# Two small experts of a mixture of experts computed in 21 short steps among the large ones, in place of four long blocks

## The chip, the cores and the metric

The kernel runs on one core of a Trainium2 chip. The metric is device microseconds (us) from the first to the last instruction of one execution, with what lies around it; several executions are timed and the median counts. The engines of the core work side by side, each through its own list of instructions in order: PE (matrix multiply; PEld is its weight load), DVE (elementwise), ACT (activations and copies), POOL, and SP, which here only issues the weight transfers (DMA).

## The reference

Two layers of a diffusion transformer on 256 latent and 256 context tokens, D_MODEL 1024. Only the end of the second layer is touched: the mixture of eight experts, of which each token takes two.

```python
def moe_swiglu(h, router, w_gate, w_up, w_down):
    ...
    top_val, top_idx = lax.top_k(logits, TOP_K)          # 2 of 8
    top_w = jax.nn.softmax(top_val, axis=-1)
    ...
    for e in range(N_EXPERTS):
        he = jax.nn.silu(t @ w_gate[e]) * (t @ w_up[e])   # 1024 -> 3584
        out = out + gates[:, e:e + 1] * (he @ w_down[e])  # 3584 -> 1024
```

All weights are float32; the eight experts' gate, up and down matrices are 352 MB, each read once.

## The kernel before

The mixture fills the second half of the span. The router sorts experts 2 to 7 by how many tokens chose them. The first six in processing order are **large**: up to 128 token rows each, computed with split weights. `eload` (L157 to L164) brings a **unit** of weights, 128 x 2048 float32 or 1 MB, into one of eight ring buffers (`w` four times, `x1w` and `zw` twice each) by a DMA on SP's queue. `wsplit` (L166) makes of each half of the unit a high part `wh` (ACT, L196) and a low part `wl` (DVE, L197); there are four buffers of each, two units' worth, so ACT and DVE can be two units ahead of PE. `mm3` (L185) then runs three matmuls: high by `wh` (L186), low by `wh` (L187), high by `wl` (L188).

The hidden width of 3584 is cut into four **pieces**: three of 1024 and one of 512 (`piece`). `up_big` does for a piece eight units of gate and up (four in the short one) into banks `mgu`: gate first, then up. `hidden` forms silu(gate) on ACT (L1810) and the product with up on DVE (L1811), tile `hd`. `turn` transposes `hd` on PE (`mht`, L1857) and splits it into `mdH` and `mdL`. `down_big` runs the down projection of the piece before (`yb`), four units. So the loop runs: gate and up of piece i, down of piece i-1, transposes of piece i. When a large expert is done, `finish` and `scatter` (`sct`) add its rows to `acc`; for every second expert `gather` (`xg`) collects the next two experts' rows.

The last two experts, the **pair**, have few tokens: 64 rows each. They share a 128-row tile: expert i's matmuls use half of PE's columns (`r = slice(64 * i, 64 * i + 64)`), unsplit, straight from the ring buffers. `up_pair` (`pgu`, L1844), `turn` with `pair` set (`mht`, tile `hTP`) and `down_pair` (`py`, L1887, sums in `yP` by L1893 and L1895) do a piece of both experts in one block of 24 units (16 of gate and up, 8 of down; half of that in the last piece). The four blocks stand in the list of tasks at fixed places:

```python
tasks = [(s, c) for s in range(PAIR) for c in range(NP)]
for c, i in zip(range(NP), (2, 8, 14, 20)):
    tasks.insert(i, (PAIR, c))
```

The code's order is not quite the engines' order: a scheduler in the framework, which estimates times when the kernel is built, lists every engine's instructions, and on the chip each engine follows its list. PSUM has four banks for gate and up (tag `gu`).

Of the kernel before, what the change touches and what calls it, by code (L numbers as in the profile page):

```python
# [17 lines left out]
P = 128  # L18
# [10 lines left out]
def build(tc, A, out, stages=("s0", "mix0", "ffn0", "mix1", "moe"), dbg=None):  # L29
# [1243 lines left out]
            T.matmul(b[:, 0:NE], ones, sel[:, t, :], start=(t == 0), stop=(t == 1))  # L1273
        V.tensor_copy(R_["cnt"], b[:, 0:NE])

    def route_order(tp, m2):


        n = NE - 2
        cnt, posm, gate = R_["cnt"], R_["posm"], R_["gate"]  # L1280
        sh = [P, n, n]

        def scr(nm):
            return m2.tile([P, n, n], F32, name="or" + nm, tag="or" + nm, bufs=1)
        a, q = scr("H"), scr("L")
        co = cnt[:, 2:].unsqueeze(1).to_broadcast(sh)
        ce = cnt[:, 2:].unsqueeze(2).to_broadcast(sh)
        V.tensor_tensor(q, co, ce, op=OP.is_equal)
        V.tensor_tensor(a, co, ce, op=OP.is_gt)
        V.tensor_tensor(q, q, R_["tie"][:, 2:, 2:], op=OP.mult)  # L1290
        V.tensor_tensor(a, a, q, op=OP.add)
        rank = tp.tile([P, n], F32, name="orank")
        V.tensor_reduce(rank, a, axis=AX.X, op=OP.add)

        one = tp.tile([P, n, n], F32, name="oone")
        V.scalar_tensor_tensor(one, rank.unsqueeze(1).to_broadcast(sh), 1.0,
                               iota[:, 0:n].unsqueeze(2).to_broadcast(sh), OP.add, OP.is_equal)

        def by_place(dst, src):
            q = scr("L")  # L1300
            V.tensor_tensor(q, one, src.unsqueeze(1).to_broadcast(sh), op=OP.mult)
            V.tensor_reduce(dst, q, axis=AX.X, op=OP.add)
        R_["posS"] = tp.tile([P, 2, n], F32, name="posS")
        R_["gateS"] = tp.tile([P, 2, n], F32, name="gateS")
        num = tp.tile([P, n], F32, name="onum")
        numi = tp.tile([P, n], I32, name="onumi")
        by_place(num, iota[:, 1:1 + n])
        V.tensor_copy(numi, num)
        for t in range(2):
            by_place(R_["posS"][:, t, :], posm[:, t, 2:])  # L1310
            by_place(R_["gateS"][:, t, :], gate[:, t, 2:])
        cap = R_["cap"] = tp.tile([P, NE], F32, name="ocap")
        G.memset(cap[:, 0:2], float(P))
        V.tensor_scalar(cap[:, 2:], rank, float(n - 2) - 0.5, -64.0, OP.is_gt, OP.mult)
        V.tensor_scalar(cap[:, 2:], cap[:, 2:], float(P), None, OP.add)
        return [nc.values_load(numi[0:1, i:i + 1], engines=[mybir.EngineType.SP], min_val=0, max_val=NE - 1)
                for i in range(n)]
# [391 lines left out]
    if "moe" in stages:  # L1709
# [27 lines left out]
        if True:  # L1737
# [64 lines left out]

                return c * 1024, min(1024, FFE - c * 1024)

            def hidden(bs):

                hds_ = []
                for g, u in zip(*bs):
                    hd = hd_tile()
                    S.activation(hd, g, AF.Silu)  # L1810
                    V.tensor_tensor(hd, u, hd, op=OP.mult)  # L1811
                    hds_.append(hd)
                return hds_

            def up_big(s, c, xH, xL, so):
                o, w = piece(c)
                nh, nk = w // 512, 2048 // w
                bs = []
                for i, W in enumerate((Wg, Wu)):
                    bb = [bank("mgu", "gu", 4) for _ in range(nh)]  # L1820
                    for u in range(KD // nk):
                        get = first.pop((s, c, i, u), None) or wsplit(eload(W, num[s], nk * u, o, w))
                        for h in range(nh):
                            for kk in range(nk):
                                k = nk * u + kk
                                mm3(bb[h], xH[:, k, so:so + P], xL[:, k, so:so + P],
                                    *get(kk * w + h * 512, 512), k == 0, k == KD - 1)
                    bs.append(bb)
                return hidden(bs)

            def up_pair(c, xP):
                o, w = piece(c)
                nh, nk = w // 512, 2048 // w
                bs = []
                for W in (Wg, Wu):
                    bb = [bank("pgu", "gu", 4) for _ in range(nh)]
                    for u in range(KD // nk):
                        ws = [eload(W, num[PAIR + i], nk * u, o, w) for i in range(2)]
                        for kk in range(nk):
                            k = nk * u + kk  # L1840
                            for h in range(nh):
                                for i in range(2):
                                    r = slice(64 * i, 64 * i + 64)
                                    T.matmul(bb[h][r], xP[:, k, r], ws[i][:, kk * w + h * 512:kk * w + h * 512 + 512],  # L1844
                                             start=(k == 0), stop=(k == KD - 1))
                    bs.append(bb)
                return hidden(bs)

            def turn(hds_, pair):

                n = 512 * len(hds_)
                dH = m2.tile([P, 1024], F32 if pair else F32R, tag="mdH", name="hTP" if pair else "mdH", bufs=1)
                dL = None if pair else m2.tile([P, 1024], F32R, tag="mdL", name="mdL", bufs=1)
                for j, hd in enumerate(hds_):
                    b = bank("mht", "mt", 1)
                    for f in range(4):
                        T.transpose(b[:, f * P:(f + 1) * P], hd[:, f * P:(f + 1) * P], ident)  # L1857
                    cs = slice(j * 512, (j + 1) * 512)
                    if pair:
                        S.activation(dH[:, cs], b, AF.Copy)  # L1860
                    else:
                        split_to(dH[:, cs], dL[:, cs], b)
                return dH, dL

            def down_big(s, c, dH, dL, yb):
                o, w = piece(c)
                for u in range(w // 256):
# [4 lines left out]
                    for f2, h in order:  # L1872
# [1 line left out]
                        fs = slice(f * P, (f + 1) * P)  # L1874
                        mm3(yb[h], dH[:, fs], dL[:, fs], *get(f2 * 1024 + h * 512, 512),
                            c == 0 and f == 0, c == NP - 1 and f == w // P - 1)

            def down_pair(c, hT, yP):
                o, w = piece(c)
                bb = [bank("py", "gu", 4) for _ in range(2)]  # L1880
                for u in range(w // 256):
                    ws = [eload(Wd, num[PAIR + i], o // P + 2 * u, 0, 1024) for i in range(2)]
                    for f2 in range(2):
                        f = 2 * u + f2
                        for h in range(2):
                            for i in range(2):
                                T.matmul(bb[h][64 * i:64 * i + 64], hT[:, f * P + 64 * i:f * P + 64 * i + 64],  # L1887
                                         ws[i][:, f2 * 1024 + h * 512:f2 * 1024 + (h + 1) * 512],
                                         start=(f == 0), stop=(f == w // P - 1))
                for h in range(2):  # L1890
                    cs = slice(h * 512, (h + 1) * 512)
                    if c:
                        V.tensor_tensor(yP[:, cs], bb[h], yP[:, cs], op=OP.add)  # L1893
                    else:
                        S.activation(yP[:, cs], bb[h], AF.Copy)  # L1895

            def scatter(acc, s, yH, yL):
                for t in range(2):
# [25 lines left out]
            xs_, SelT, ybs = {}, {}, {}  # L1924
            xs_[0] = gather(0)
            dump("lg", R_["lg"])
            tasks = [(s, c) for s in range(PAIR) for c in range(NP)]
            for c, i in zip(range(NP), (2, 8, 14, 20)):
                tasks.insert(i, (PAIR, c))
            tasks.append(None)  # L1930
            pend, done, yP = None, [], None
            for i, task in enumerate(tasks):
                hd_ = None
                if task is not None:
                    s, c = task
                    if s == PAIR:
                        hd_ = up_pair(c, xP)
                    else:
                        if c == 0:
                            ybs[s] = [bank("yb", "yb") for _ in range(2)]  # L1940
                        hd_ = up_big(s, c, *xs_[s // 2], (s % 2) * P)
                for d in done:
                    scatter(acc, *d)
                done = []
                if pend is not None:
                    (s1, c1), d1 = pend
                    if s1 == PAIR:
                        if c1 == 0:
                            yP = m2.tile([P, D], F32, name="yP", bufs=1)
                        down_pair(c1, d1[0], yP)  # L1950
                        if c1 == NP - 1:
                            done.append(finish(PAIR, yP))
                    else:
                        down_big(s1, c1, *d1, ybs[s1])
                        if c1 == NP - 1:
                            done.append(finish(s1, ybs.pop(s1)))
                pend = (task, turn(hd_, s == PAIR)) if task is not None else None
                if i == 0:
                    route_gates(mp, m2)
                    dump("gate", gate)  # L1960
                    num += route_order(mp, m2)
                    xP, gp = gather_pair()
                if i == 1:
                    acc = mp.tile([P, 2, D], F32, tag="acc", name="acc")
                    G.memset(acc, 0.0)
# [123 lines left out]
```

## Time and profile before

| what | us |
|---|---|
| median of three runs | 2022.61 (2021.28 to 2024.07) |
| the profiled execution | 2018.54 |
| its span, first to last instruction | 2016.8 |
| of which mixture of experts, first `mgu` to last `yb` | about 1047 to 1999 |
| PE busy over the span | 1860.4 |

Busy PE time is to be read with care: a matmul's row lasts longer than the distance to the next one, since they overlap. Work is therefore priced below by the distance between starts.

### The profile page before, as it was taken

What the parts mean: (1) busy time and instruction counts of PE and PEld (TensorE: products, weight loads), DVE (VectorE), ACT (ScalarE), POOL (GpSimd) and SP (SyncE); (2) the same over time, 40 slices, a digit from 0 to 9 for tenths busy, and PEclk for the clock granted to TensorE, in tenths of its full rate; (3) what the DMA queues carried; (4) which work ended last, traced back from release to release, by engine and by line L of the source; (5) the groups of instructions that cost most, each with busy time, mean ns of one, the idle gap of its engine ahead of it and who ended that gap; (6) DMA issues with size and microseconds to landing.
All of it is one profiled execution on the core that took longest, in us unless ns stands there. A gap on an engine that the chain in (4) does not pass through costs nothing. (4 is left out here: it accounts for less than half of the span.)

```text
span 2016.8 us, 25616 instructions
## 1 busy us (share of the span) xinstructions
PE 1860.4 (92%) x9278; PEld 1369.1 (68%) x9278; DVE 1394.2 (69%) x2054; ACT 1037.2 (51%) x1492; POOL 160.2 (8%) x144
## 2 busy tenths in 40 slices
PE   5999999989999999865879999999999999999996
PEld 2667667867777787655658467846785687567775
DVE  6575775688875476486778358935883588578886
ACT  3522355543333365325466347724772477457765
POOL 1000310001111001055220000000000000000000
PEclk9999999989999999887979999999999999999998
DMA  9474314436666656637557999899999999999992
GB/s 350 162 261 149 134 42 176 160 112 212 219 209 201 221 188 245 233 121 272 211 223 261 368 409 397 332 356 410 405 368 378 413 384 360 340 385 352 355 336 109
DMA packets 196970, 545.55 MB, mean 271 GB/s; under 512 B 32620, under 2 KB 62421, under 8 KB 189285
## 3 DMA queue, kind: packets, MB, share of 16 engines
q1 hardware_dynamic: 165884, 514.73, 68.2%
q10 hardware_dynamic: 29400, 23.50, 4.0%
q0 software_dynamic: 1552, 5.62, 1.0%
q8 instruction: 75, 1.23, 0.2%
q14 instruction: 59, 0.48, 0.1%
HBM read 517.85 MB, written 25.89 MB: 270 GB/s over the span
## 5 line engine op out<-in xcount | busy, mean ns | idle before, releaser
L197 DVE TENSOR_TENSOR wl<-w,wh 128x1024 fp32r<-128x1024 f32 x380 | 449.7, 1224 | 101.7 <-ACT wh L196 98.9
L196 ACT ACTIVATE wh<-w 128x1024 fp32r<-128x1024 f32 x390 | 395.4, 1055 | 190.8 <-PE dn L187 49.0
L186 PE MATMUL mgu<-wh,xgH 128*128 128x512 f32 x448 | 178.4, 399 | 0.0
L187 PE MATMUL mgu<-wh,xgL 128*128 128x512 f32 x448 | 176.8, 396 | 0.0
L188 PE MATMUL mgu<-wl,xgH 128*128 128x512 f32 x448 | 168.4, 399 | 0.9 <-DVE wl L197 0.7
L196 ACT ACTIVATE wh<-zw 128x1024 fp32r<-128x1024 f32 x122 | 124.3, 1057 | 53.5 <-DMA zw<-in_od_moe_w_down_dram 29.3
L197 DVE TENSOR_TENSOR wl<-x1w,wh 128x1024 fp32r<-128x1024 f32 x122 | 142.9, 1218 | 11.4 <-ACT wh L196 11.0
L186 PE MATMUL gu<-hH,wh 128*128 128x512 f32 (+1 forms) x384 | 146.9, 383 | 2.2 <-ACT hH L196 2.2
L197 DVE TENSOR_TENSOR wl<-zw,wh 128x1024 fp32r<-128x1024 f32 x122 | 142.4, 1218 | 7.9 <-ACT wh L196 7.6
L188 PE MATMUL gu<-hL,wh 128*128 128x512 f32 (+1 forms) x384 | 145.2, 379 | 0.0
L187 PE MATMUL gu<-hH,wl 128*128 128x512 f32 (+1 forms) x384 | 144.3, 376 | 0.0
L196 ACT ACTIVATE wh<-x1w 128x1024 fp32r<-128x1024 f32 x124 | 126.0, 1056 | 19.6 <-PE yb L187 6.9
L186 PE MATMUL yb<-wh,mdH 128*128 128x512 f32 x336 | 133.5, 398 | 0.7 <-ACT mdH L196 0.7
L187 PE MATMUL yb<-wh,mdL 128*128 128x512 f32 x336 | 132.4, 394 | 0.0
L188 PE MATMUL yb<-wl,mdH 128*128 128x512 f32 x336 | 116.0, 400 | 11.6 <-DVE wl L197 11.6
L188 PEld LDWEIGHTS mgu<-wl,xgH 128*128 128x128 f32 x448 | 84.5, 189 | 23.8 <-DVE wl L197 4.1
L186 PEld LDWEIGHTS mgu<-wh,xgH 128*128 128x128 f32 x448 | 84.7, 189 | 20.0 <-ACT wh L196 1.0
L187 PEld LDWEIGHTS mgu<-wh,xgL 128*128 128x128 f32 x448 | 84.7, 189 | 18.9
L186 PE MATMUL mgu<-wh,xB 128*128 128x512 f32 x224 | 88.2, 394 | 2.0 <-ACT wh L196 2.0
L186 PEld LDWEIGHTS gu<-hH,wh 128*128 128x128 f32 x384 | 73.6, 192 | 20.2 <-issue 5.9
L187 PE MATMUL mgu<-wh,xB 128*128 128x512 f32 x224 | 87.1, 392 | 0.0
L188 PE MATMUL mgu<-wl,xB 128*128 128x512 f32 x224 | 82.7, 394 | 0.1
(722 smaller groups left out, 3775.1 us busy)
## 6 DMA issues: line engine op xcount, KB each, us to landing
w<-in_od_moe_w_up_dram SPq DMA_DIRECT2D x56, 1024.0 KB
w<-in_od_moe_w_gate_dram SPq DMA_DIRECT2D x55, 1024.0 KB
w<-in_od_moe_w_down_dram SPq DMA_DIRECT2D x54, 1024.0 KB
w<-in_ada_w_dram SPq DMA_DIRECT2D x48, 1024.0 KB
zw<-in_od_moe_w_down_dram SPq DMA_DIRECT2D x31, 1024.0 KB
x1w<-in_od_moe_w_up_dram SPq DMA_DIRECT2D x29, 1024.0 KB
x1w<-in_od_moe_w_gate_dram SPq DMA_DIRECT2D x28, 1024.0 KB
x1w<-in_od_moe_w_down_dram SPq DMA_DIRECT2D x27, 1024.0 KB
```

Source lines behind the costliest of these rows:

```text
L186: T.matmul(b, aH, bH, start=start, stop=False)
L187: T.matmul(b, aL, bH, start=False, stop=False)
L188: T.matmul(b, aH, bL, start=False, stop=stop)
L196: S.activation(h, src, AF.Copy)
L197: (eng or V).tensor_tensor(l, src, h.bitcast(F32), op=OP.subtract)
```

## The change

The pair is done in 21 **steps**: for each of seven chunks of 512 of the hidden width a gate step (`pair_gate`), a hidden step (`pair_hidden`, the up projection and the product) and a down step (`pair_down`). Each takes four units, two per expert, and 16 matmuls. The step runs inside `up_big`, between gate and up of a large expert's piece, through the callback `mid`, from the third piece on: 21 steps in pieces 3 to 23 of 24. The gate activation of the large piece now stands in the code ahead of `mid`. The transposes of the pair's hidden tile (`pair_turn`, `pht`) are put behind the up projection of the piece by the list `late`. The pair has its own tiles `hdP` (hidden), `hTP` (transposed) and `yP`; the scratch of `route_order` lies in `hdP`. Sums, operands and the number of matmuls and of bytes stay what they were; the pair's gate and up units are now four rows of 512 per partition each, and not two of 1024.

```diff
-            def up_big(s, c, xH, xL, so):
+            def up_big(s, c, xH, xL, so, mid):
...
+                    for h in range(nh):
+                        if i == 0:
+                            hds_.append(hd_tile())
+                            S.activation(hds_[h], bb[h], AF.Silu)
+                        else:
+                            V.tensor_tensor(hds_[h], bb[h], hds_[h], op=OP.mult)
+                    if i == 0:
+                        mid()
+                return hds_
+
+            def pair_up(q, W):
+
+                b = bank("pgu", "gu", 4)
+                for u in range(2):
+                    ws = [eload(W, num[PAIR + i], 4 * u, q * 512, 512) for i in range(2)]
+                    for kk in range(4):
+                        k = 4 * u + kk
+                        for i in range(2):
+                            r = slice(64 * i, 64 * i + 64)
+                            T.matmul(b[r], xP[:, k, r], ws[i][:, kk * 512:(kk + 1) * 512],
+                                     start=(k == 0), stop=(k == KD - 1))
+                return b
+
+            def pair_gate(q):
+                S.activation(hdP, pair_up(q, Wg), AF.Silu)
+
+            def pair_hidden(q):
+                V.tensor_tensor(hdP, pair_up(q, Wu), hdP, op=OP.mult)
+                late.append(pair_turn)
+
+            def pair_turn():
+                b = bank("pht", "mt", 1)
+                for f in range(4):
+                    T.transpose(b[:, f * P:(f + 1) * P], hdP[:, f * P:(f + 1) * P], ident)
+                S.activation(hTP, b, AF.Copy)
+
+            def pair_down(q):
+                bb = [bank("py", "gu", 4) for _ in range(2)]
+                for u in range(2):
+                    ws = [eload(Wd, num[PAIR + i], q * 4 + 2 * u, 0, 1024) for i in range(2)]
+                    for f2 in range(2):
+                        f = 2 * u + f2
+                        for h in range(2):
+                            for i in range(2):
+                                T.matmul(bb[h][64 * i:64 * i + 64], hTP[:, f * P + 64 * i:f * P + 64 * i + 64],
+                                         ws[i][:, f2 * 1024 + h * 512:f2 * 1024 + (h + 1) * 512],
+                                         start=(f == 0), stop=(f == 3))
+                for h in range(2):
+                    cs = slice(h * 512, (h + 1) * 512)
+                    if q:
+                        V.tensor_tensor(yP[:, cs], bb[h], yP[:, cs], op=OP.add)
+                    else:
+                        S.activation(yP[:, cs], bb[h], AF.Copy)
...
-            for c, i in zip(range(NP), (2, 8, 14, 20)):
-                tasks.insert(i, (PAIR, c))
...
+            steps = [(f, q) for q in range(FFE // 512) for f in (pair_gate, pair_hidden, pair_down)]
+            pend, done, late = None, [], []
+
+            def mid():
+                if i > 1 and steps:
+                    f, q = steps.pop(0)
+                    f(q)
...
+                    hd_ = up_big(s, c, *xs_[s // 2], (s % 2) * P, mid)
+                    if late:
+                        late.pop()()
+                    if steps == []:
+                        steps = None
+                        done.append(finish(PAIR, yP))
```

Three places in the engines' lists. A name is written out<-in, and the number behind a name tells one buffer's use from the next.

The first is ACT's list between gate and up of the second piece of the second large expert. Before, the two silu rows `hd` of the gate stand between splits of up weights:

```order
L196 ACTIVATE wh_10454<-x1w_8441 128x1024
L196 ACTIVATE wh_10458<-x1w_8441 128x1024
L196 ACTIVATE wh_10477<-x1w_8441 128x1024
L196 ACTIVATE wh_10481<-x1w_8441 128x1024
L1810 ACTIVATE hd_10563<-mgu_10387 128x512
L1810 ACTIVATE hd_10566<-mgu_10388 128x512
L196 ACTIVATE wh_10499<-w_10497 128x1024
L196 ACTIVATE wh_10503<-w_10497 128x1024
```

After, in the same piece, which holds a gate step of the pair (`wh_10371` and `wh_10375` are the last gate unit, `wh_10421` and `wh_10425` the first up unit):

```order
L196 ACTIVATE wh_10371<-w_10369 128x1024
L196 ACTIVATE wh_10375<-w_10369 128x1024
L1822 ACTIVATE hd_10391<-mgu_10302 128x512
L1822 ACTIVATE hd_10393<-mgu_10303 128x512
L1843 ACTIVATE hdP_9073<-pgu_10395 128x512
L196 ACTIVATE wh_10421<-x1w_8441 128x1024
L196 ACTIVATE wh_10425<-x1w_8441 128x1024
L196 ACTIVATE wh_10443<-w_10441 128x1024
```

The pair's silu, which reads the sum that PE has just finished, has come to stand ahead of the split of the first up unit, and the first up unit's split has moved behind the large piece's silu rows.

The second is DVE's list at gate and up of the third piece of the third large expert. Before, splits of the last two gate units and of the first two up units follow each other:

```order
L197 TENSOR_TENSOR wl_11981<-w_11978,wh_11980 128x1024
L197 TENSOR_TENSOR wl_11985<-w_11978,wh_11984 128x1024
L197 TENSOR_TENSOR wl_12002<-zw_8607,wh_12001 128x1024
L197 TENSOR_TENSOR wl_12006<-zw_8607,wh_12005 128x1024
L197 TENSOR_TENSOR wl_12025<-zw_8607,wh_12024 128x1024
L197 TENSOR_TENSOR wl_12029<-zw_8607,wh_12028 128x1024
L197 TENSOR_TENSOR wl_12046<-x1w_8441,wh_12045 128x1024
L197 TENSOR_TENSOR wl_12050<-x1w_8441,wh_12049 128x1024
```

After, the piece holds a down step:

```order
L197 TENSOR_TENSOR wl_11872<-w_11869,wh_11871 128x1024
L197 TENSOR_TENSOR wl_11876<-w_11869,wh_11875 128x1024
L197 TENSOR_TENSOR wl_11893<-zw_8607,wh_11892 128x1024
L197 TENSOR_TENSOR wl_11897<-zw_8607,wh_11896 128x1024
L1869 TENSOR_TENSOR yP_9219<-py_11916,yP_9219 128x512
L1869 TENSOR_TENSOR yP_9219<-py_11917,yP_9219 128x512
L197 TENSOR_TENSOR wl_11946<-w_11943,wh_11945 128x1024
L197 TENSOR_TENSOR wl_11950<-w_11943,wh_11949 128x1024
```

Two sums that read the step's result stand between the split of the last gate unit and that of the first up unit.

The third is PE's list in the piece ahead of that one, which after the change holds a hidden step: the last pair matmuls, then the transposes of `hdP`, then the first up unit.

```order
L1838 MATMUL pgu_11586<-x1w_8441,xP_9166 64x512
L1838 MATMUL pgu_11586<-w_11598,xP_9166 64x512
L1852 MATMUL pht_11700<-cpk_76,hdP_9073 128x128 x4
L186 MATMUL mgu_11609<-wh_11613,xB_10626 128x512
L187 MATMUL mgu_11609<-wh_11613,xB_10626 128x512
L186 MATMUL mgu_11610<-wh_11613,xB_10626 128x512
L187 MATMUL mgu_11610<-wh_11613,xB_10626 128x512
L188 MATMUL mgu_11609<-wl_11614,xB_10626 128x512
```

Before, gate and up follow each other there without a row between:

```order
L188 MATMUL mgu_11633<-wl_11705,xB_10686 128x512
L187 MATMUL mgu_11634<-wh_11704,xB_10686 128x512
L188 MATMUL mgu_11634<-wl_11705,xB_10686 128x512
L186 MATMUL mgu_11720<-wh_11724,xB_10686 128x512
L187 MATMUL mgu_11720<-wh_11724,xB_10686 128x512
```

The transposes have been listed directly behind the step, though the code has them behind the up projection.

## Rows read from the trace of the kernel before

**Rows 1.** Windows: us; PE, PEld, DVE, ACT, POOL busy (x); PEclk; DMA share, GB/s.

```profile
1108.60:1219.90 111.30, 107.97 (x462) 64.27 (x460) 54.51 (x51) 48.82 (x55) 0.00 (x0) 0.98 0.98 391
...
1326.00:1402.10 76.10, 72.38 (x305) 36.16 (x304) 23.99 (x24) 21.44 (x26) 0.00 (x0) 1.00 0.98 388
...
1527.10:1608.40 81.30, 78.81 (x341) 43.41 (x340) 32.27 (x34) 25.86 (x31) 0.00 (x0) 1.00 1.00 401
...
1735.70:1816.00 80.30, 77.25 (x317) 47.12 (x317) 50.63 (x53) 40.08 (x47) 0.00 (x0) 1.00 0.93 365
...
1046.80:1999.20 952.40, 926.06 (x4061) 666.14 (x4060) 681.16 (x699) 575.17 (x644) 1.81 (x1) 1.00 0.93 356
```

**Rows 2.** Windows, one stretch behind the first block, the same columns.

```profile
1200.00:1230.00 30.00, 30.00 (x133) 24.25 (x132) 25.64 (x24) 22.17 (x23) 0.00 (x0) 1.00 1.03 415
```

**Rows 3.** Groups by line and form on PE, 1046.8 to 1999.2.

```profile
L188 PE MATMUL yb<-wl,mdH 128*128 128x512 f32 x336 | 116.0, 400 | 11.6 <-DVE wl L197 11.6
...
L1844 PE MATMUL pgu<-w,xP 128*64 128x512 f32 x224 | 73.9, 597 | 1.4 <-DMA w<-in_od_moe_w_up_dram 1.4
```

**Rows 4.** Timeline, PE: start, us, form, count; a down block begins.

```profile
1383.24 0.39 PE L187 MATMUL mgu<-wh,xgL 128*128 128x512 f32 x1
1383.47 0.39 PE L188 MATMUL mgu<-wl,xgH 128*128 128x512 f32 x1
1383.79 1.93 PE L1887 MATMUL py<-w,hTP 128*64 128x512 f32 x4
1385.65 0.33 PE L1857 MATMUL mht<-cpk,hd 128*128 128x128 f32 x1
```

**Rows 5.** Timeline inside a block, both halves of PE at work.

```profile
1749.94 0.59 PE L1844 MATMUL pgu<-zw,xP 128*64 128x512 f32 x1
...
1749.94 0.59 PE L1844 MATMUL pgu<-x1w,xP 128*64 128x512 f32 x1
...
1750.37 0.59 PE L1844 MATMUL pgu<-zw,xP 128*64 128x512 f32 x1
```

**Rows 6.** Timeline: a down block ends, ACT and DVE follow, then `mgu`.

```profile
1398.60 1.94 PE L1887 MATMUL py<-w,hTP 128*64 128x512 f32 x8
...
1400.58 0.60 ACT L196 ACTIVATE mdH<-mht 128x512 fp32r<-128x512 f32 x1 [19.75 <-PE py L1887]
1400.58 0.69 DVE L1893 TENSOR_TENSOR yP<-py,yP 128x512 f32<-128x512 f32 x1 [0.17 <-PE py L1887]
1401.07 2.00 ACT L196 ACTIVATE wh<-w 128x1024 fp32r<-128x1024 f32 x2
...
1402.15 2.36 DVE L197 TENSOR_TENSOR wl<-w,wh 128x1024 fp32r<-128x1024 f32 x2 [0.25 <-ACT wh L196]
...
1402.17 0.50 PE L186 MATMUL mgu<-wh,xB 128*128 128x512 f32 x1 [1.63 <-ACT wh L196]
...
1403.43 0.50 PE L188 MATMUL mgu<-wl,xB 128*128 128x512 f32 x1
```

**Rows 7.** Timeline: a product on DVE, and the transposes that read it.

```profile
1556.63 0.69 DVE L1811 TENSOR_TENSOR hd<-pgu,hd 128x512 f32<-128x512 f32 x1 [27.96 <-PE pgu L1844]
...
1557.38 0.66 PE L1857 MATMUL mht<-cpk,hd 128*128 128x128 f32 x4
```

**Rows 8.** Timeline: transposes, then `yb` at the end of an up projection.

```profile
1243.27 0.60 PE L1857 MATMUL mht<-cpk,hd 128*128 128x128 f32 x4
...
1244.78 0.73 PE L188 MATMUL yb<-wl,mdH 128*128 128x512 f32 x2 [0.91 <-DVE wl L197]
```

**Rows 9.** Timeline, PE: a block broken by a scatter.

```profile
1739.06 2.79 PE L1844 MATMUL pgu<-w,xP 128*64 128x512 f32 x10
1741.78 0.50 PE L1903 MATMUL sct<-ym,SelT 128*128 128x512 f32 x1
```

**Rows 10.** Windows around the end of the first down block, columns as above.

```profile
1190.00:1195.00 5.00, 3.10 (x15) 1.11 (x11) 1.00 (x2) 2.97 (x5) 0.00 (x0) 1.00 1.05 387
1195.00:1200.00 5.00, 4.65 (x15) 3.40 (x14) 5.00 (x6) 4.00 (x6) 0.00 (x0) 0.66 1.04 399
```

More of the change, by code (lines that the diff above doesn't have):

```diff
@@ L1274, in route_gates, with route_order @@
         V.tensor_copy(R_["cnt"], b[:, 0:NE])
-    def route_order(tp, m2):
+    def route_order(tp, room):
         n = NE - 2
@@ L1283, in scr @@
         def scr(nm):
-            return m2.tile([P, n, n], F32, name="or" + nm, tag="or" + nm, bufs=1)
+            return room[:, 64 * "HL".index(nm):][:, 0:n * n].rearrange("p (a b) -> p a b", a=n)
         a, q = scr("H"), scr("L")
@@ L1803, in piece @@
                 return c * 1024, min(1024, FFE - c * 1024)
[L1805 to L1813, printed above, removed]
-            def up_big(s, c, xH, xL, so):
+            def up_big(s, c, xH, xL, so, mid):
                 o, w = piece(c)
                 nh, nk = w // 512, 2048 // w
-                bs = []
+                hds_ = []
                 for i, W in enumerate((Wg, Wu)):
@@ L1827, in up_big @@
                                     *get(kk * w + h * 512, 512), k == 0, k == KD - 1)
[L1828 to L1853, printed above, removed]
+                    for h in range(nh):
[4 more added lines that the diff above has]
+                            V.tensor_tensor(hds_[h], bb[h], hds_[h], op=OP.mult)
@@ L1854, in turn @@
+            def turn(hds_):
+                dH, dL = [m2.tile([P, 1024], F32R, tag="md" + n, name="md" + n, bufs=1) for n in "HL"]
                 for j, hd in enumerate(hds_):
@@ L1857, in turn @@
                         T.transpose(b[:, f * P:(f + 1) * P], hd[:, f * P:(f + 1) * P], ident)
[L1858 to L1862, printed above, removed]
+                    split_to(dH[:, j * 512:(j + 1) * 512], dL[:, j * 512:(j + 1) * 512], b)
                 return dH, dL
@@ L1876, in down_big @@
                             c == 0 and f == 0, c == NP - 1 and f == w // P - 1)
[L1878 to L1895, printed above, removed]
             def scatter(acc, s, yH, yL):
@@ L1926, in build @@
             dump("lg", R_["lg"])
-            tasks = [(s, c) for s in range(PAIR) for c in range(NP)]
-            for c, i in zip(range(NP), (2, 8, 14, 20)):
-                tasks.insert(i, (PAIR, c))
-            tasks.append(None)
-            pend, done, yP = None, [], None
+            tasks = [(s, c) for s in range(PAIR) for c in range(NP)] + [None]
+            steps = [(f, q) for q in range(FFE // 512) for f in (pair_gate, pair_hidden, pair_down)]
[4 more added lines that the diff above has]
+                    f(q)
             for i, task in enumerate(tasks):
@@ L1935, in build @@
                     s, c = task
[L1936 to L1941, printed above, removed]
+                    if c == 0:
+                        ybs[s] = [bank("yb", "yb") for _ in range(2)]
+                    hd_ = up_big(s, c, *xs_[s // 2], (s % 2) * P, mid)
[4 more added lines that the diff above has]
+                        done.append(finish(PAIR, yP))
                 for d in done:
@@ L1946, in build @@
                     (s1, c1), d1 = pend
[L1947 to L1957, printed above, removed]
+                    down_big(s1, c1, *d1, ybs[s1])
+                    if c1 == NP - 1:
+                        done.append(finish(s1, ybs.pop(s1)))
+                pend = (task, turn(hd_)) if task is not None else None
                 if i == 0:
@@ L1960, in build @@
                     dump("gate", gate)
-                    num += route_order(mp, m2)
+                    hdP = m2.tile([P, 512], F32, name="hdP", bufs=1)
+                    num += route_order(mp, hdP)
                     xP, gp = gather_pair()
+                    yP = m2.tile([P, D], F32, name="yP", bufs=1)
+                    hTP = m2.tile([P, 512], F32, name="hTP", bufs=1)
                 if i == 1:
```

## The prediction, on record before the run

> **What bounds the kernel now.** I read the windows first, over the mixture of experts and over its four stretches around the pair's blocks [rows 1]: PE is busy 926 of 952 us, DVE 681, ACT 575, the DMA engines 0.93 of the time at 356 GB/s. PE is the bound on the whole, but not by much: behind a block the DMA share stands at 1.03 with 415 GB/s [rows 2], so at best one 1.05 MB unit lands in 2.53 us. The groups by line [rows 3] say what PE waits for: 11.6 us in `yb` for the low part `wl` from DVE, and little for weights still in flight (1.4 us in the largest group of `pgu`).
>
> Busy time hides lost time, so I price PE by distances. A split matmul costs 0.233 us (two starts 0.23 apart) [rows 4]. Each pair matmul is two rows of the trace; two halves side by side start together and the next two 0.43 later [rows 5], so a row costs 0.214 us. With these, the four stretches of [rows 1] last 111.3 + 76.1 + 81.3 + 80.3 = 349.0 us and hold 1425 PE rows. Counted in the timeline, 672 are the pair's (144.0 us), 653 are split matmuls (152.1), 72 are transposes (6.3) and 28 scatters and gathers (5.6): 308.0 us. **So the blocks now lose some 41 us.** That is all the change can win. The other stretches lose about 17 us, nearly all of it at ends of up projections.
>
> What a piece asks for, even demand assumed: a full piece is 12 units, 144 split matmuls, 33.6 us of PE against 12 x 2.53 = 30.4 us of DMA. With a step it is 16 units, 40.5 us of DMA, against 33.6 + 6.9 (32 rows x 0.214) = 40.5 us plus every wait below. A block alone asks for 16 units (40.5 us) within 27.4 us of PE. So DMA is over-asked in a block and not in a step; eight ring buffers cover the difference of single pieces.
>
> **What the change adds, step by step.** It removes the blocks with their 41 us. Matmuls, transposes and bytes stay; four terms come back.
>
> (1) *Order of the halves.* When two matmuls of one half follow each other, the other half idles: four rows in a row cost 1.86 us and not 0.86 [rows 4]. The `py` rows of a step still begin so. Walking the PE list with 0.857 us for a matmul on its half, the steps take 156.0 us where 144.0 would be perfect: 12.0 us. (The blocks, walked alike, take 157.7; that 13.7 lies in the 41.)
>
> (2) *Entries and exits.* From a split matmul into pair work 0.32 instead of 0.23 [rows 4], and a first pass of 0.48: 0.15 us. The list now has 32 stretches of pair matmuls, since scatters and gathers cut some steps; there were 21. 32 x 0.15 = 4.8 us. Leaving one in its middle costs at most 0.2 more: ten rows, that is five matmuls, three of them on one half, take 2.72 to the scatter, where 3 x 0.857 = 2.57 would do [rows 9]; 11 x 0.2 = 2.2 us.
> A rule speaks here against cutting work up: the Trainium skill, "TensorEngine Tiling (Array Packing)", Key Properties, says that a change of tiling mode drains the engine. Its word alone would price an exit at the rest of the last row, 0.59 - 0.43 = 0.16 us, and the whole term at 6.6 us instead of 7.0; the rows agree that the price is small.
>
> (3) *Waits behind a step.* This is the large term. In the lists of the changed kernel an instruction that reads the step's result stands ahead of the first up unit's split, so that this split starts only when the step is over. Three kinds:
> - *Gate* (7): on ACT the pair's silu, then `wh`. The end of a down block has the same shape: the last `py` pair starts at 1399.95 (1398.60 + 1.94 - 0.59), ACT gets its 0.60 us row in at 1400.58, `wh` at 1401.07, PE its next matmul at 1402.17: 2.22 us where 0.43 is due. Then `wl` takes 1.2 more and L188 starts 1403.43, 0.2 late [rows 6]. 2.0 us for full pieces, 2.5 in the short one, where L188 comes after two matmuls and not four. The first step has up splits listed ahead of its silu: 0.2. Sum 5 x 2.0 + 2.5 + 0.2 = 12.7 us.
> - *Hidden* (7): on DVE the product, on PE directly behind the step the transposes `pht`, which need it. A product takes 0.69, and the transposes start 0.06 behind its end [rows 7]; it starts 0.63 behind the last pair row's start, as ACT's row did [rows 6]. 0.63 + 0.69 + 0.06 - 0.43 = 0.95 us; `wl` is then ready in time, except in the short piece (0.3 more). The first has neither row in the way: 0.2. Sum 5 x 0.95 + 1.2 + 0.2 = 6.2 us.
> - *Down* (7): on DVE two sums, then `wl`. The second sum runs 1400.58 to 1401.27 [rows 6]; `wl` would end 1.22 later, 1402.49, while PE, `wh` being ready, could reach L188 at 1400.5 + 4 x 0.233 = 1401.4. So 1.15 us, 1.65 in each of two short pieces; the first, with copies on ACT, is like a gate step, 2.0; one has seven gather matmuls in between, 0.35; the last must wait for sums, scaling and two splits before its scatter, 2.4. Sum 3.3 + 2.0 + 0.35 + 2.4 + 2.3 = 10.3 us.
> Together 29.2 us. Bounds: if nothing is late, an exit alone costs 0.16, 21 x 0.16 = 3.4 us; if every step is like the worst row, 21 x 2.5 = 52 us. I take the middle one, since both engines work their lists in order here and each kind has a row of its own shape.
>
> (4) *Ends of up projections.* There DVE's product for the large piece stands ahead of `wl`, and PE stands 1.1 us (1.51 from the transposes to `yb` where 0.41 would do) [rows 8]. The list has this shape 12 times before and 15 times now, as three of the old places were at blocks: 3 x 1.1 = 3.3 us.
>
> Sum: 12.0 + 7.0 + 29.2 + 3.3 = 51.5 us come back, 41 go: **10 us slower**. The profiled execution took 2018.5 us, 4.1 below the median of 2022.6; added to the median: **2032.6 us**. The cause in one line: the blocks starved on DMA only a little, and each step adds a round trip PE to ACT or DVE and back.
>
> **Rivals.**
> *The waits are covered, and it is faster.* If PE waits less than 0.7 us per step on average, 14.7 in place of 29.2, 37 us come back and the kernel is 4 us faster; at the lower bound 51.5 - 25.8 = 25.7, 15 us faster, 2007 us. For it: `wh` and `wl` have two units of room, and DMA is no longer over-asked. Against: the room lies behind the blocked instruction, not ahead of it.
> *Nothing to tell.* Within 4 us (0.2%, what three runs of this kernel can tell from no change): waits of about 0.7 to 1.1 per step, 2018.6 to 2026.6.
> *The clock falls.* Behind the first down block PE is busy 3.1 of 5 us, and in the next 5 us the granted clock is 0.66 on average, 1.2 GHz instead of 2.4 for part of it [rows 10]: (1 - 0.66) x 5 = 1.7 us lost. One of four block ends did this. Now eight places wait about 2 us: at one in four 2 falls, at worst eight, 8 x 1.7 - 1.7 = 12 us more, 2044 us. The Trainium skill, "TensorE: Matmul & The Clock Gate", Part 1, says that idle gaps bring the slow clock back; the one fall agrees.
> *DMA becomes the bound.* The pair's 56 gate and up units are now rows of 512. If they move at 387 GB/s, as such rows did around 1190 at a share of 1.05 [rows 10], each costs 2.7 us, 10 us more transfer in all, against the 48 us of waits and switches that PE adds. Only if slack in single pieces runs out, 5 us on top, 2037.
>
> **Chances.** The forecast, 4 to 20 us slower: 0.58. No difference: 0.20. Waits covered, faster: 0.14. Over 20 us slower (clock, DMA): 0.08. So faster 0.14, same 0.20, slower 0.66. The range reaches from 2017 (a small part of the faster case) to 2043 (10 us above, five or six falls of the clock); the forecast's own is 2026.6 to 2042.6.
>
> **What would show it.** Right: behind gate steps PE idles 1.6 us or more until `wh`, behind hidden steps about 0.9 until the product, behind down steps about 1 until `wl`; no wait of `pgu` or `py` for DMA; DMA below its 1.03 throughout, near 370 GB/s. The silu `hdP` starts 0.6 us behind the last `pgu` start, and `wh` follows at once. Wrong: PE goes on into the up projection without a gap, so that the list's order doesn't matter; or DMA waits appear in steps; or ends of up projections lose much more or less than 1.1 us each.

## The result and the profile after

The changed kernel took 2032.44 us (median of 5 runs, 2031.22 to 2036.49), the kernel before beside it 2021.28 us (2019.91 to 2024.07). The ratio is **1.0059, 95% interval 1.0043 to 1.0074**: some 11 us slower, where 10 were forecast. The profiled execution is the median run; its span is 2030.5 us, 13.7 above the 2016.8 of the kernel before.

The windows of the changed kernel: the whole mixture, and four stretches around one gate step (the columns of [rows 1]).

```profile
1047.80:2011.50 963.70, 925.37 (x4060) 659.39 (x4058) 685.33 (x703) 578.96 (x643) 1.81 (x1) 0.99 0.92 352
1485.00:1490.00 5.00, 5.00 (x25) 2.38 (x25) 0.65 (x2) 0.60 (x1) 0.00 (x0) 1.00 1.04 412
1490.00:1495.00 5.00, 4.02 (x20) 1.14 (x16) 0.00 (x0) 0.90 (x2) 0.00 (x0) 1.00 0.78 291
1495.00:1500.00 5.00, 3.79 (x10) 2.73 (x11) 4.33 (x4) 4.42 (x5) 0.00 (x0) 0.75 1.03 416
1500.00:1505.00 5.00, 5.00 (x21) 4.05 (x21) 2.56 (x4) 3.38 (x4) 0.00 (x0) 0.91 1.02 419
```

PE has the same work (925 us busy, 926 in [rows 1]), but the mixture is 13 us longer: the windows end at different places (that of [rows 1] 2 us behind the last `yb`, this one 0.4 us), and from the first `mgu` to the end of the last `yb` it takes 950.2 us before and 963.3 after. DMA is asked for less per microsecond, not more (352 GB/s, 356 before). What PE waited for most, from 1108 to 2012 (engine, line, what it waited for: us in total, times, longest):

```profile
PE yb L188 <- DVE wl L197: 13.4, 15, 0.9
PE mgu L186 <- ACT wh L196: 12.1, 8, 1.7
PE pht L1852 <- DVE hdP L1846: 4.9, 6, 0.8
PE mgu L188 <- DVE wl L197: 4.6, 5, 1.2
```

The first row was there before [rows 3]. The other three are new or grew, and each is one kind of step: `wh` behind gate steps, the product behind hidden steps, `wl` behind down steps. No row has `pgu` or `py` waiting for DMA. One gate step in the timeline (start, us, engine, line, operation, in brackets the idle time before it and what ended it):

```profile
1493.43 0.59 PE L1838 MATMUL pgu<-x1w,xP 128*64 128x512 f32 x1
...
1494.10 0.60 ACT L1843 ACTIVATE hdP<-pgu 128x512 f32<-128x512 f32 x1 [6.46 <-PE pgu L1838]
1494.59 2.00 ACT L196 ACTIVATE wh<-x1w 128x1024 fp32r<-128x1024 f32 x2
...
1495.67 2.36 DVE L197 TENSOR_TENSOR wl<-x1w,wh 128x1024 fp32r<-128x1024 f32 x2 [10.02 <-ACT wh L196]
...
1495.69 0.50 PE L186 MATMUL mgu<-wh,xB 128*128 128x512 f32 x1 [1.67 <-ACT wh L196]
...
1496.95 0.51 PE L188 MATMUL mgu<-wl,xB 128*128 128x512 f32 x1 [0.52 <-DVE wl L197]
...
1497.57 0.63 PE L187 MATMUL mgu<-wh,xB 128*128 128x512 f32 x1
```

The reader is to see ACT's 6.46 us of idling before `hdP`: the split was not late for lack of weights or of a buffer, but because the silu ahead of it in ACT's list waited for PE. The last row shows what followed: at 1497 a split matmul begins to take 0.63 and not 0.39, and the granted clock is 0.75 and 0.91 in the two windows above. Between full speed and half, that is (0.25 + 0.09) x 5 = 1.7 us lost. Three steps of the changed kernel have such a fall (at 1497, 1627 and 1955), the kernel before has one in the mixture [rows 10]. The windows behind the other two:

```profile
1626.00:1632.00 6.00, 5.94 (x18) 4.51 (x19) 6.00 (x6) 4.93 (x6) 0.00 (x0) 0.72 1.02 417
...
1955.00:1960.00 5.00, 5.00 (x17) 3.96 (x16) 5.00 (x6) 3.92 (x5) 0.00 (x0) 0.67 1.02 410
```

### The profile page after: what moved, and what is told of

Same layout as the page of the kernel before. It is cut to its first block, busy times and chain, and to the rows that moved or that the text cites. A ratio compares the mean times of both kernels' runs of the same rounds, so it can differ in the third digit from the quotient of the medians.

```text
span 2030.5 us, 25587 instructions
## 1 busy us (share of the span) xinstructions
PE 1860.4 (92%) x9278; PEld 1363.0 (67%) x9278; DVE 1399.9 (69%) x2060; ACT 1041.9 (51%) x1492; POOL 160.2 (8%) x144
## 5 line engine op out<-in xcount | busy, mean ns | idle before, releaser
L196 ACT ACTIVATE wh<-x1w 128x1024 fp32r<-128x1024 f32 x126 | 129.5, 1056 | 33.1 <-PE mgu L187 15.9
L188 PE MATMUL yb<-wl,mdH 128*128 128x512 f32 x336 | 119.3, 400 | 13.4 <-DVE wl L197 13.4
L186 PEld LDWEIGHTS mgu<-wh,xgH 128*128 128x128 f32 x448 | 84.5, 189 | 33.8 <-ACT wh L196 11.6
```

Of the source, the lines that this page charges most:

```text
L186: T.matmul(b, aH, bH, start=start, stop=False)
L188: T.matmul(b, aH, bL, start=False, stop=stop)
L196: S.activation(h, src, AF.Copy)
```

## The experiments

All ratios are against the kernel before, timed beside on the same chip (its medians: 2020.2 us for r1 to r4, 2020.6 for r5 to r8, 2021.8 for r9 and r10).

**r1, r2, r3: the readers queued later.** In r1 the instruction that reads a step's result is written behind the split of the second up unit and held there in its engine's list (`keep` orders an instruction behind those written before it on its engine and adds no wait):

```diff
 get = first.pop((s, c, i, u), None) or wsplit(eload(W, num[s], nk * u, o, w))
+if i and u == 1:
+    read()
...
-S.activation(hdP, pair_up(q, Wg), AF.Silu)
+b = pair_up(q, Wg)
+readers.append(lambda: keep(S.activation(hdP, b, AF.Silu)))
...
-V.tensor_tensor(hdP, pair_up(q, Wu), hdP, op=OP.mult)
+b = pair_up(q, Wu)
+readers.append(lambda: keep(V.tensor_tensor(hdP, b, hdP, op=OP.mult)))
```

and the same for the two sums or copies of `pair_down`; `read()` writes out the readers gathered so far. r2 has only the first of these edits (gate), r3 only the others (hidden, down).

> The instructions that read a step's result (silu of the gate, product, sums) are queued on ACT and DVE behind the splits of the first two up units; nothing else is changed. If the waits behind the steps come from these places in the lists (gate 17.8, hidden 7.1, down 12.6 us in the changed kernel's trace, 37.5 in all, clock falls in them included), only 0.2 to 0.3 us per step is left of them: about 30 us less, 2002 us, no fall of the clock behind a step, and the waits of mgu and yb for wh and wl go. If transfers are the real limit (share 0.94 already), the time hardly falls, 2022 to 2030 us, the share goes to 1.0 and pgu, py or wh wait for DMA. If the clock alone costs, 5 us less, 2027.

> The same, only for the seven gate steps (silu of the pair behind the splits of two up units on ACT). Waits theory: 17.8 us less 7 times 0.3, 15 us less, 2017 us, with the falls of the clock behind steps 9 and 12 gone. Rival (transfers): no more than 3 us less. By the sizes in the prediction, without the clock: 11 us less, 2021.

> The same, only for the seven hidden and seven down steps (product and sums behind the splits of two up units on DVE, in the first down step the copies on ACT). Waits theory: 7.1 and 12.6 us less 14 times 0.2, 16 us less, 2016 us. Together with the gate steps alone this should give what all of them give. Rival (transfers): no more than 3 us less.

| kernel | median us | ratio, interval | span profiled |
|---|---|---|---|
| r1 all late | 2002.40 | 0.9911 (0.9895 to 0.9928) | 1999.7 |
| r2 gate late | 2015.32 | 0.9975 (0.9965 to 0.9985) | 2012.3 |
| r3 hidden, down late | 2016.89 | 0.9982 (0.9973 to 0.9992) | 2012.4 |

The waits theory gave 2002, 2017 and 2016. What PE waited for in r1, the same stretch of the mixture:

```profile
PE yb L188 <- DVE wl L197: 13.2, 15, 0.9
PE xg L1756 <- DVE acc L1913: 0.8, 1, 0.8
PE yb L186 <- ACT mdH L196: 0.7, 1, 0.7
```

In r2, where hidden and down steps keep their readers in front:

```profile
PE pht L1855 <- DVE hdP L1849: 4.9, 6, 0.8
PE mgu L188 <- DVE wl L197: 4.1, 4, 1.2
PE mgu L186 <- ACT wh L196: 2.2, 2, 1.6
```

In r3, where the gate steps do:

```profile
PE mgu L186 <- ACT wh L196: 10.0, 6, 1.7
...
PE mgu L188 <- DVE wl L197: 0.5, 1, 0.5
```

Each edit takes away its own rows and leaves the others. The same gate step in r1's timeline:

```profile
1483.14 0.59 PE L1840 MATMUL pgu<-x1w,xP 128*64 128x512 f32 x1
1483.66 0.50 PE L186 MATMUL mgu<-wh,xB 128*128 128x512 f32 x1
...
1483.81 0.60 ACT L1846 ACTIVATE hdP<-pgu 128x512 f32<-128x512 f32 x1 [2.68 <-PE pgu L1840]
1484.00 0.40 PE L187 MATMUL mgu<-wh,xB 128*128 128x512 f32 x1
```

The silu still follows the step by 0.67 us, but PE goes on after 0.52 instead of 2.26, since the splits ahead of it were done during the step. Transfers did not stop this: the rival that they are the limit (2022 or more) is out.

**r4: the halves of a step alternate.** Step (1) of the prediction, on its own: the pair's matmuls keep the code's order on PE, ABAB, and ACT's and DVE's readers stay where the change put them.

```diff
+def one(m):
+    tc.stamp_issue_order_token(m.ins, "pair")
...
-T.matmul(b[r], xP[:, k, r], ws[i][:, kk * 512:(kk + 1) * 512],
-         start=(k == 0), stop=(k == KD - 1))
+one(T.matmul(b[r], xP[:, k, r], ws[i][:, kk * 512:(kk + 1) * 512],
+             start=(k == 0), stop=(k == KD - 1)))
```

> The pair's matmuls are kept in the order of the code on PE, so that the two halves alternate everywhere (ABAB), where the changed kernel's py rows begin AABB; ACT's and DVE's lists keep the readers where they are. By step (1) of the prediction each AABB costs a matmul's time on one half: walked that way the steps go from 156.0 to 150.0 us, 6 us less, 2026 us. If each half works off its own list, and only unequal counts in a stretch cost, nothing or 1 us either way: 2031 to 2033.

Median 2029.90 us, ratio 1.0055 (1.0035 to 1.0075): the changed kernel's 1.0059. The pair's rows lose 29.5 us beyond 0.214 each in the changed kernel and 29.4 here. The 2.5 us between the medians are no more than the clock explains: one fall behind these steps where the changed kernel has three. The reason stands in the changed kernel's own timeline, at the begin of a down step whose order is AABB:

```profile
1325.65 4.08 PE L1863 MATMUL py<-w,hTP 128*64 128x512 f32 x17
...
1329.57 0.59 PE L1863 MATMUL py<-w,hTP 128*64 128x512 f32 x1
```

Less the last row's 0.59, 17 rows start within 3.49 us, 0.218 per row: full rate in spite of AABB. The same step in r4, where the halves alternate, has the same row (that the order did change shows in the uncut down steps, which lose 0.22 us beyond 0.214 per row in the changed kernel and 0.17 in r4):

```profile
1325.94 4.08 PE L1866 MATMUL py<-w,hTP 128*64 128x512 f32 x17
```

In [rows 4] four rows took 1.86 us because transposes came behind them: that stretch had only one half's matmuls in it.

**r5, r6: half the pair's bytes**, with all readers late and in the kernel before: `ws = [eload(W, num[PAIR], ...)] * 2` in place of a unit for each expert, so that the second expert is computed with the first one's weights.

> All readers late as in r1, and each pair unit is loaded for the first small expert only and used for both (the output is not the reference's): 84 of 1.05 MB less to fetch, same matmuls. If waits behind steps are all that the changed kernel lost, and transfers keep up in r1 too, the time stays at r1's 2002 us, within 3. If r1 already runs into the transfers, 10 us or more less.

> The kernel before with the pair's units loaded for the first small expert only and used for both (not the reference's output). By the prediction the blocks starve on transfers only a little: of the 41 us no more than 5 come back, 2015 us or more. Rival: the blocks, at share 1.03, are bound by transfers: 15 us or more less, 2005.

r5 took 1980.82 us, 0.9796 (0.9776 to 0.9816); r6 1977.72 us, 0.9786 (0.9769 to 0.9803). Each fetched 42 units less, 501.5 MB in place of 545.5 (the 84 above is all of the pair's units). Both expectations missed. Read as written, both runs say that transfers are the limit. They don't show it, since the lists moved: with fewer transfers the scheduler, which estimates them, places other instructions differently. r5 has 21 uncut stretches of pair matmuls, where r1 has 32; its pair rows lose 3.3 us and not 11.2; and its waits at ends of up projections fell as well:

```profile
PE yb L188 <- DVE wl L197: 5.3, 7, 0.9
```

These two make 7.9 + 7.9 of the 21.6 us between r1 and r5. In r6 the same row went from 11.6 to 4.7, and the pair's rows from 28.6 us lost to 5.7 in lists that alternate nearly everywhere. An experiment on bytes has to hold the lists still, and these two don't; I count them as inconclusive. What they won can be had without saving a byte, though: from the first `mgu` to the end of the last `yb`, r5 takes 910.4 us and r6 909.9, and r10 below, with all bytes, 910.7. Its waits of `yb` are 3.0 us shorter than r5's (2.3 and 5.3), so the bytes are worth some 3 us at most there, not 20.

**r7: late readers in the kernel before**, silu and product of the pair behind the second unit's splits in the down projection that follows, sums behind the second unit's splits of the next gate projection.

```diff
-S.activation(hd, g, AF.Silu)
-V.tensor_tensor(hd, u, hd, op=OP.mult)
+if pair:
+    def act(g=g, u=u, hd=hd):
+        keep(S.activation(hd, g, AF.Silu))
+        keep(V.tensor_tensor(hd, u, hd, op=OP.mult))
+    readers.append(act)
...
 get = wsplit(eload(Wd, num[s], o // P + 2 * u, 0, 1024))
+if u == 1:
+    read()
```

> The kernel before, four blocks, with the readers of the pair's results (silu, product, sums) behind the splits of two units, as in r1. If the round trip at a block's end is the same mechanism, its seven ends (2 us at a down block's, less at an up block's) and the fall of the clock at 1196 give 8 to 10 us back, 2011 us, so that the steps with late readers (2002) are still ahead by the rest of the 41. Rival: blocks with late readers reach 2002 too, then the cutting into steps is worth nothing by itself.

Median 2019.93 us, ratio 0.9993 (0.9979 to 1.0006): no change, where 2011 was expected. The end of the first down block in r7's timeline:

```profile
1194.74 0.60 ACT L196 ACTIVATE mdH<-mht 128x512 fp32r<-128x512 f32 x1 [20.95 <-PE py L1897]
1195.23 1.05 ACT L196 ACTIVATE wh<-w 128x1024 fp32r<-128x1024 f32 x1
...
1196.12 0.66 PE L1865 MATMUL mht<-cpk,hd 128*128 128x128 f32 x4 [1.41 <-DVE mdL L197]
...
1196.53 0.48 PE L186 MATMUL mgu<-wh,xgH 128*128 128x512 f32 x1
```

ACT stood still again, for 20.95 us, now ahead of the large expert's own `mdH`; `wh` came behind it, PE's transposes waited for the `mdL` that follows `mdH`, and the clock fell as before. `mdH` does not read the block's result: the transposes that it copies had run by 1181. It waits for its buffer, which in the kernel before is also that of the pair's `hTP`:

```python
dH = m2.tile([P, 1024], F32 if pair else F32R, tag="mdH", name="hTP" if pair else "mdH", bufs=1)
```

So `mdH` can't be written before the last `py` has read `hTP`, wherever the readers stand. The change gives `hTP` a buffer of its own, a part of it that the prediction doesn't price. r7 therefore doesn't test the theory for blocks. What blocks with late readers and a separate `hTP` would give wasn't tried.

**r8: the large experts' product late too.** On top of r1, DVE's product of gate and up stands behind the split of the first down unit.

```diff
-V.tensor_tensor(hds_[h], bb[h], hds_[h], op=OP.mult)
+prods.append(lambda b=bb[h], d=hds_[h]: keep(V.tensor_tensor(d, b, d, op=OP.mult)))
...
 get = wsplit(eload(Wd, num[s], o // P + 2 * u, 0, 1024))
+if u == 0:
+    multiply()
```

> r1, and the large experts' own product of gate and up is queued on DVE behind the split of the first down unit. The waits at the ends of up projections (13.2 us in r1, 15 places of 0.9) are of the same kind, so they should go: 2002 less 13, 1989 us. Rival: the transposes then come late and md is late for the next down projection: no gain.

Median 1986.50 us, ratio 0.9824 (0.9807 to 0.9841). Of the 13.2 us in 15 places one place is left:

```profile
PE yb L188 <- DVE wl L197: 0.9, 1, 0.9
```

The gain over r1 is 15.9 us, 12.3 of it these listed waits.

**r9: the halves alternate in the kernel before** (the edit of r4 in `up_pair` and `down_pair`).

> The kernel before, with the pair's matmuls kept in the order of the code on PE, so that the halves alternate in all blocks (all weights fetched). If the order of the halves is a large part of the 41 us that the blocks lose (13.7 us by the prediction, walked 157.7 to 150.8 us), it gets 6 to 8 us faster, 2013 us. If each half works off its own list and the blocks' pair rows are slow for lack of weights, within 3 us of 2020.

Median 2014.76 us, ratio 0.9965 (0.9952 to 0.9978): 7 us less, about what was expected if the order counts; the profiled spans differ by 2.5. So order does cost something in the blocks, whose `py` began with one half's two matmuls and then transposes, but the pair's rows still lose 25.4 us of 28.6. r9 also waits more for weights, 5.5 us against 2.6:

```profile
PE pgu L1847 <- DMA zw<-in_od_moe_w_up_dram: 2.9, 2, 1.5
PE pgu L1847 <- DMA w<-in_od_moe_w_up_dram: 2.2, 2, 1.5
...
PE py L1890 <- DMA w<-in_od_moe_w_down_dram: 0.4, 1, 0.4
```

**r10: no cuts.** On top of r8, scatters and gathers are held on PE behind the up projection (`end[0]` is its last matmul):

```diff
 for d in done:
-    scatter(acc, *d)
+    with tc.issue_after(end[0].ins):
+        scatter(acc, *d)
...
-xs_[task[0] // 2 + 1] = gather(task[0] // 2 + 1)
+with tc.issue_after(end[0].ins):
+    xs_[task[0] // 2 + 1] = gather(task[0] // 2 + 1)
```

> r8, and scatters and gathers are queued on PE behind the up projection in whose piece they fall, so that no step is cut (21 stretches of pair matmuls, not 32). pgu and py lose 11.2 us in r8 beyond 0.214 us per row, 0.2 in an uncut step: 7 us less, 1979 us. By step (2) of the prediction, 11 stretches at 0.15 to 0.35 us, 4 us less, 1982. Rival: the scatters only move and cost the same elsewhere, 1986.

Median **1980.39 us, ratio 0.9796 (0.9779 to 0.9814)**: 41 us below the kernel before and 52 below the changed one. The pair's rows lose 3.7 us, 11.2 in r8. The time lies between the 1979 expected from these rows and the 1982 of step (2). The window over the mixture and what is left of the waits of `yb`:

```profile
1049.50:1967.00 917.50, 908.92 (x4067) 655.87 (x4066) 694.98 (x707) 586.47 (x648) 1.81 (x1) 1.00 0.95 370
```

```profile
PE yb L188 <- DVE wl L197: 2.3, 6, 0.4
PE yb L186 <- ACT mdH L196: 0.7, 1, 0.7
```

PE is now busy 99% of this window, which ends with the last scatter, at a DMA share of 0.95.

## Why the prediction came out as it did

The size and the sign were right, the large term and its cause too; one step was wrong, and it was luck that an error the other way made up for it.

**The waits behind steps (3), forecast 29.2 us: right.** r1 takes them away and leaves the pair's 32 stretches as they were: 30.8 us by the spans (2030.5 - 1999.7), 30.0 by the medians. *Gate*, forecast 12.7: r3, which keeps them, is 12.7 above r1 in the spans (14.5 in the medians). *Hidden and down*, forecast 6.2 + 10.3 = 16.5: r2 is 12.6 above r1 (12.9 in the medians), a quarter less than forecast. 12.7 + 12.6 = 25.3; the missing 5.5 of the 30.8 are about the three falls of the clock, 3 x 1.7 = 5.1, since the profiled runs of r1, r2 and r3 have none in the mixture.

**The clock, a rival with its own chance: it came in part.** Three falls and not the two at one in four, 3.4 us net of the one before. The Trainium skill, "TensorE: Matmul & The Clock Gate", Part 1, says that idle gaps bring the slow clock back. The three falls do follow waits of PE: 1.67 us at 1494 and at 1624, and three short ones from 1952 to 1954 (0.68, 0.29 and 0.52). But the profiled run of r3 has six gate waits of up to 1.7 us and no fall, and that of r4 seven and one fall. Each is a single execution: r3's ten go from 2014.14 us at a mean granted clock of 0.971, the profiled one, to 2019.28 at 0.966, so the number of falls seems to differ between executions of one kernel. What decides which gap does it stays open.

**The order of the halves (1), forecast 12.0 us: wrong.** I walked the list as if PE had to start its matmuls strictly in order, so that AABB blocks B. The row of 17 above and r4 show that it doesn't: a half runs ahead of the other, and r4, which by the same walk was to win 6 us, won nothing that the clock doesn't explain. What does cost is a stretch in which one half has more to do than the other, and those are made by the cuts.

**Entries and exits (2), forecast 7.0 us: too low.** Cuts alone cost about as much: with 11 stretches fewer r10 saves 7.5 us in the pair's rows (6.1 in the median), some 0.6 for each where I had 0.35. An uncut step loses 0.18 in its own rows (3.7 / 21 in r10), 0.09 in the row ahead (0.32 for 0.23 [rows 4]) and 0.11 in the row behind (1483.66 to 1484.00 in r1's rows above, 0.34 for 0.23): 0.38 in all where I took 0.15. Together (1) and (2) measure 11.2 + 32 x 0.20 = 17.6 us in r1 against the 19.0 forecast: the two errors nearly cancel.

**Ends of up projections (4), forecast 3.3 us.** The listed wait grew by 1.8 us (11.6 to 13.4), in 15 places before and after, where I had counted 12 before. The term is small, but the 12 to 13 us that both kernels lost there were the next largest thing to win, as r8 shows.

**The blocks' 41 us.** Without the waits the steps would win 41 - 12.0 - 7.0 - 3.3 = 18.7 us by the prediction; r1's span is 17.1 below that of the kernel before. So the sum holds, though not each of its terms. Added up from the starts of PE's rows, from the first `mgu` to the last `yb`, the pair's rows take 172.6 us before and 155.3 in r1, all other rows 777.2 and 777.6: what is won is won in the pair's rows, which lose 28.6 of the 41. PE's waits before, behind the first row of [rows 3]:

```profile
PE mht L1857 <- DVE mdL L197: 3.6, 3, 1.9
PE mgu L186 <- ACT wh L196: 2.0, 2, 1.6
PE pgu L1844 <- DMA w<-in_od_moe_w_up_dram: 1.4, 2, 0.8
PE pgu L1844 <- DMA zw<-in_od_moe_w_up_dram: 1.2, 2, 0.6
PE mht L1857 <- DVE hd L1811: 0.9, 1, 0.9
```

Of the 28.6, some 6 are waits at ends of blocks (3.4 of the first row, 1.6 of the second, the last), 2.6 are listed as waits for weights, and 3 to 7 go by alternating (r9). The weights may cost more than is listed: the three long stretches of up projections (122, 124 and 128 rows) lose 9.1 us before, 8.8 in r9 and 1.5 in r6 (122, 122 and 128 rows), some 7.5 us with all bytes, if r6's other lists don't matter there. That still fits "starved on DMA only a little". The rest is not settled.

**The other rivals.** "Waits covered, faster" was wrong for the change as made, and its condition, less than 0.7 us per step, is what r1 sets up by other means: 2002 us, below the 2007 that I had given for it. "DMA becomes the bound" did not come: no step waits for weights, and r10 moves the same bytes in a mixture of 910.7 us instead of 963.3. One sign failed all the same: DMA was to stay below 1.03 and near 370 GB/s, and it stood at 1.04 in the first window at the gate step and at 352 GB/s on the whole.

## What to carry to other kernels

An engine's list is a queue: an instruction that waits for the latest result holds back all that is ready behind it, so when work is cut into more pieces, count the readers of each piece's result and queue them behind the work that the next piece needs. Cutting the blocks was worth 18 us (with late readers, and with a separate buffer for `hTP`), and the place of 21 readers cost 30. Ask first whether the instruction that blocks a list reads a late result or waits for a shared buffer, as `mdH` does in r7: moving readers helps only the first. And when an experiment changes what a scheduler believes (bytes, durations), compare the lists before the times.

## What the runs showed that I had not expected

The two halves of PE's columns do not hold each other up: in the order AABB 17 rows start 0.218 us apart on average, as in ABAB, while a stretch of four rows on one half before other work takes 1.86 us, both in the changed kernel (at 1570) and in [rows 4].

A late reader costs nearly nothing, although the pair's bank is held longer: in r1 PE goes from the last pair matmul to the next split matmul in 0.52 us.

The clock falls behind some gaps of about 1.7 us and not behind others of the same size: three falls in the changed kernel's profiled run, one of them behind shorter waits, one in r4's, none in r3's, which has six such gaps.
